# Attention values in one pass of four heads, the compressed branch interleaved with projections, five staging tiles, last sums by part

## The chip, the cores and the metric

The kernel runs on one core of a Trainium2 chip. The metric is the time of one execution in device microseconds (us); a comparison goes by medians of runs. The engines are TensorE (PE in the rows, PEld its weight loads), VectorE (DVE), ScalarE (ACT), GpSimd (POOL) and SyncE (SP), which here only issues transfers. [...]

## What is computed

One layer of a hybrid decoder block for 1024 tokens of width 1024, all in float32, and a last RMSNorm. Cut to what matters here:

```python
h = rmsnorm(x, norm1_g); proj = h @ w_in           # one joint input projection
q, kv, gate, qkv, z, b, a = split(proj)            # 8 NSA heads in 2 groups, 4 GDN heads
k_cmp = rope(kv[:, :, 0])
o_cmp, p = nsa_compressed(q, k_cmp, kv[:, :, 1])   # blocks of 32 tokens every 16, a small MLP:
                                                   #   silu((blk + cmp_pos) @ w1) @ w2
o_slc = nsa_selected(q, k_slc, v_slc, top8(p))     # 64-token blocks chosen by p
o_win = nsa_window(q, k_win, v_win)                # the last 512 tokens
o_nsa = rmsnorm(g0*o_cmp + g1*o_slc + g2*o_win)
o_gdn = gated_deltanet(conv_silu(qkv), b, a) * silu(z)
x = x + concat(o_nsa, o_gdn) @ w_out
x = x + (silu(rmsnorm(x) @ w_gate) * (rmsnorm(x) @ w_up)) @ w_down
return rmsnorm(x, final_g)
```

## The kernel before

**Products in two parts.** Every float32 operand of a large product is split into a high and a low part (`xh`/`xl`, or the two halves of a weight tile), and `split3` (lines 119 to 121) makes one product of three matmuls: high by high, high by low, low by high. `wprep` (L195) brings a weight in: it loads chunks of 512 columns into staging tiles `wraw` (three buffers), ScalarE makes the high part (L205), POOL the low one (L208).

**Order.** The code is written stage by stage, and a scheduler then places the instructions on each engine's queue. Nothing overtakes on a queue. All transfers are issued by SyncE's queue, so a store that waits for its data holds up every load behind it.

**Stages**, with their place in the span. 0 to 61 us: `proj_tok(0)` and `proj_tok(1)`, projections to tokens in rows, eight groups of 24 matmuls each. `proj_tok(0)`'s weights `w0` come with the tiles of x through three staging tiles `xraw`, k by k (L235 to L242); their results go out through `zt` to `zD` (L252, L253). Beside them x is read once more by tokens (`in_xN`, L265) for the norm, and VectorE and ScalarE make sine and cosine of the positions (`ang`, L305; `sn`, L307). 61 to 90 us: `proj_tok(2)`, the keys and values of the compressed branch, whose groups `evac_cmp` (L329) scales into `ck` on ScalarE and rotates on POOL. 90 to 108 us: the compressed branch. `cmp_blocks` transposes the `ck` tiles (L340) and spreads them to `kdt` (L345 on VectorE, L346 on ScalarE); four additions of the block positions (L360) on VectorE; for each of the keys and the values 16 products (L365), a tanh (L369), a small product (L375, L384). 108 to 330 us: `gdn_proj`, twelve gated projections with a convolution on VectorE, the later ones between the GDN chunks' Gram matrices. 330 to 428 us the GDN scan, then the attention's keys. 480 to 785 us: the attention, in 16 units (8 token tiles by 2 groups), of which more below. Then `w_out`, the gate and up projections, and the down projection to 1466 us; after it the sums of squares of the last norm and the result's last tokens.

**Attention units.** `scores(u)` fills probabilities `PC` (compressed), `Pw` (window) and `Ps` (selected) for four heads; `values(u)` (L1029) multiplies them with the values. It takes two heads at a time: for each pair of heads and each key block, TensorE transposes into bank `b` (L1059 for PC, L1065), ScalarE copies the high part to `PT` (L1067), VectorE subtracts the low part (L1068), and TensorE adds products of 256 columns in bank `c` (L1045), of which there is one buffer. After a pair's last block ScalarE copies half of `c` to `otmp` (L1049) and VectorE adds the other half into `mn` (L1050); only then can the next pair's products enter `c`. `merge` weaves the streams of scores, values and output projection (`wob`) by estimated costs `wa` and `wc`.

**Tail.** `norm_sum` (L1606) sums squares over the partitions by products with ones, token chunk by token chunk (L1611), VectorE scales the sum (L1614), POOL takes the power (L1615), TensorE spreads it (L1621), and VectorE and POOL scale the last tokens, which leave in two transfers of 512 KB (L1663).

## Time and profile before

| | |
|---|---|
| median of 3 runs | 1499.25 us (1497.87 to 1504.8) |
| the profiled execution | 1494.86 us |
| its span, first to last instruction | 1493.1 us |
| mean granted clock of TensorE in it | 0.985 |
| TensorE busy | 1426.7 us, 96% |
| VectorE, ScalarE, POOL busy | 65%, 48%, 47% |

The span lies inside the execution's time; all rows below are from this one execution. A busy TensorE is not a TensorE at its peak, since the ends of matmuls are modelled and they overlap: the distance from one start to the next is what one costs. A share in brackets behind a row is idle time of the engine just ahead of it and the instruction that released it.

### The profile page before, as it was taken

The numbers are of one execution on the slowest core, as the hardware profiler recorded it, in microseconds if no ns is written. First come the engines' busy times: TensorE is split into PE (matmuls) and PEld (weight loads), VectorE is DVE, ScalarE is ACT, GpSimd is POOL, SyncE is SP. The second block draws the span as 40 slices with busy tenths as digits, with TensorE's granted clock in tenths as the row PEclk, the third lists the DMA queues.
The fourth block names the chain that finished last, engine by engine and source line by source line (L and its number), as shares of the span: only waits on it lengthen the run. The fifth ranks groups of instructions, "written<-read, shape, count | busy, mean of one in ns | idle before, by whom it ended". The sixth has DMA issues, their size and how long they took to land.

```text
span 1493.1 us, 23452 instructions
## 1 busy us (share of the span) xinstructions
PE 1426.7 (96%) x7984; PEld 1220.1 (82%) x7984; DVE 966.9 (65%) x2286; ACT 723.5 (48%) x1604; POOL 708.1 (47%) x755
## 2 busy tenths in 40 slices
PE   8889999999998999999999999999999999999997
PEld 8878877899987887888887788888888887888886
DVE  4326688826655898998956864444444434999955
ACT  5433356236655888778755543333333332444423
POOL 1232244561121755654467277566666553345435
PEclk9999999999998999999999999999999999999998
DMA  7822255477735313101137123222222237534003
GB/s 250 300 68 78 92 171 162 126 194 208 203 119 202 101 54 107 47 22 44 36 123 244 36 87 99 83 78 85 78 86 85 85 92 274 200 119 134 1 0 113
DMA packets 142743, 174.96 MB, mean 117 GB/s; under 512 B 26912, under 2 KB 79392, under 8 KB 142496
## 3 DMA queue, kind: packets, MB, share of 16 engines
q1 hardware_dynamic: 142624, 173.47, 37.0%
q8 instruction: 63, 1.03, 0.3%
q14 instruction: 56, 0.46, 0.1%
HBM read 122.01 MB, written 51.41 MB: 116 GB/s over the span
## 4 chain that ended last, share of the span: by engine, by line
PE 60%; DVE 10%; issue 5%; ACT 5%; POOL 4%; DMA 2%; SPq 0%; POOLq 0%; ACTq 0%; DVEq 0%
PE mm L119 16%; PE mm L121 16%; PE mm L120 16%; PE c L1045 3%; PE b L1065 2%; DVE PT L1068 2%; ACT Ps L1016 1%; PE a L637 1%; DVE cy L429 1%; PE a L999 1%; PE a L644 1%; ACT PT L1067 1%; DMA wraw<-in_w_out 1%; POOL w L208 1%; DMA mgt<-mgD 1%
## 5 line engine op out<-in xcount | busy, mean ns | idle before, releaser
L1202 POOL TENSOR_TENSOR A<-wq,A 128x512 fp32r<-128x512 f32 x94 | 126.4, 1346 | 97.8 <-ACT A L1201 76.5
L1201 ACT ACTIVATE A<-wq 128x512 fp32r<-128x512 f32 x96 | 60.1, 630 | 135.0 <-PE mm L121 118.3
L119 PE MATMUL mm<-w,xh 128*128 128x256 f32 x384 | 112.2, 292 | 6.3 <-ACT w L205 3.9
L1068 DVE TENSOR_TENSOR PT<-b,PT 128x512 fp32r<-128x512 f32 (+2 forms) x168 | 103.8, 621 | 18.8 <-ACT PT L1067 17.0
L120 PE MATMUL mm<-w,xh 128*128 128x256 f32 x384 | 112.0, 292 | 1.0 <-POOL w L208 1.0
L121 PE MATMUL mm<-w,xl 128*128 128x256 f32 x384 | 111.9, 291 | 0.0
L1202 POOL TENSOR_TENSOR wk<-wq,wk 128x512 fp32r<-128x512 f32 x61 | 82.6, 1355 | 53.0 <-ACT wk L1201 44.7
L1067 ACT ACTIVATE PT<-b 128x512 fp32r<-128x512 f32 (+2 forms) x168 | 89.0, 538 | 37.4 <-PE b L1065 33.2
L1045 PE MATMUL c<-PT,vs 128*128 128x256 f32 x528 | 92.9, 300 | 0.1
L208 POOL TENSOR_TENSOR w<-wraw,w 128x512 fp32r<-128x512 f32 x48 | 63.5, 1337 | 60.6 <-ACT w L205 34.6
L1201 ACT ACTIVATE wk<-wq 128x512 fp32r<-128x512 f32 x63 | 39.6, 630 | 85.4 <-PE mm L121 78.5
L119 PEld LDWEIGHTS mm<-w,xh 128*128 128x128 f32 x384 | 75.3, 196 | 6.9 <-ACT w L205 4.1
L119 PE MATMUL mm<-T,A 128*128 128x512 f32 x200 | 79.2, 396 | 0.0
L120 PE MATMUL mm<-T,A 128*128 128x512 f32 x200 | 79.2, 396 | 0.0
L121 PE MATMUL mm<-T,A 128*128 128x512 f32 x200 | 79.2, 396 | 0.0
L1479 POOL TENSOR_TENSOR ring<-ring,ring 128x512 f32<-128x512 f32 x44 | 58.2, 1324 | 40.1 <-DVE ring L1464 26.5
L120 PEld LDWEIGHTS mm<-w,xh 128*128 128x128 f32 x384 | 75.5, 196 | 1.3 <-POOL w L208 1.2
L119 PE MATMUL mm<-xh,w 128*128 128x512 f32 x192 | 75.7, 394 | 0.0
L121 PEld LDWEIGHTS mm<-w,xl 128*128 128x128 f32 x384 | 75.4, 196 | 0.1
L121 PE MATMUL mm<-xh,w 128*128 128x512 f32 x192 | 75.3, 392 | 0.0
L1045 PEld LDWEIGHTS c<-PT,vs 128*128 128x128 f32 x528 | 73.0, 192 | 2.5 <-DVE PT L1068 0.3
L120 PE MATMUL mm<-xl,w 128*128 128x512 f32 x192 | 74.9, 390 | 0.0
(471 smaller groups left out, 4515.0 us busy)
## 6 DMA issues: line engine op xcount, KB each, us to landing
wq<-in_w_gu SPq DMA_DIRECT2D x92, 256.0 KB, 2.7
aD<-ring SPq DMA_DIRECT2D x44, 256.0 KB, 2.2
ring<-aD SPq DMA_DIRECT2D x44, 256.0 KB, 4.1
raw<-in_w_dn SPq DMA_DIRECT2D x36, 256.0 KB, 3.9
qk<-gD SPq DMA_DIRECT2D x16, 512.0 KB, 4.8
wraw<-in_w_out SPq DMA_DIRECT2D x28, 256.0 KB, 2.8
wraw<-in_w_tok SPq DMA_DIRECT2D x24, 256.0 KB, 2.9
wraw<-in_w_gdn SPq DMA_DIRECT2D x24, 256.0 KB, 2.8
```

The lines of the kernel that those rows point to most:

```text
L119: after(mm(ps, lhsT=lh, rhs=rh, start=first, stop=False, skip_group_check=grow), prev)
L120: mm(ps, lhsT=lh, rhs=rl, start=False, stop=False, skip_group_check=grow)
L121: return mm(ps, lhsT=ll, rhs=rh, start=False, stop=last, skip_group_check=grow)
L208: (lo or G).tensor_tensor(out=wt[:, 1, k0:k0 + n, :], in0=raw, in1=f32(wt[:, 0, k0:k0 + n, :]), op=ALU.subtract)
L429: V.scalar_tensor_tensor(out=y, in0=cr[:, j:j + 512], scalar=cw[:, j:j + 1], in1=y, op0=ALU.mult, op1=ALU.add)
L1045: mm(po[:, 0:256], lhsT=v, rhs=PT[0:K, a, b_ * 256:(b_ + 1) * 256], start=(n_ == 0 and a == 0), stop=(last and b_ == len(vs) - 1 and a == 1))
L1065: tpose(pt[:, o_:o_ + P], src[:, hh, b * P:(b + 1) * P], ident)
L1067: act(out=PT[0:K, 0, 0:w], in_=pt[0:K, 0:w], func=AF.Copy)
L1068: V.tensor_tensor(out=PT[0:K, 1, 0:w], in0=pt[0:K, 0:w], in1=f32(PT[0:K, 0, 0:w]), op=ALU.subtract)
L1201: act(out=dst[:, 0], in_=src, func=AF.Copy)
L1202: after(eng.tensor_tensor(out=dst[:, 1], in0=src, in1=f32(dst[:, 0]), op=ALU.subtract), prev)
L1479: G.tensor_tensor(out=t, in0=half[o], in1=t, op=ALU.mult)
```

## The change

- **Lead.** The first x tile comes as two halves of 512 columns, `w0`'s first weights between them. `xraw` has five buffers, and `w0`'s staging is a tile of its own, `w0raw`, with five. `wprep` has four staging buffers where a caller does not name a number.
- **Compressed branch.** Its weights (`w1t`, 2 MB), `w2t` and `cpt` are loaded ahead of `proj_tok(2)` in the code. `cmp_blocks(i-1)` is called in `evac_cmp(i)`; the additions of positions are 16 of 128x256, half of them on POOL. `gdn_proj(0)` stands before the large products, `gdn_proj(4)` between them and the tanh; both use the earlier pool of banks. The zero stores to `uD` and `tD` come after these.
- **Values.** One pass of four heads for each unit: products of 512 columns, half as many; one copy of 64x512 and two additions at the end of a unit instead of two copies and two additions. `Ps` has four buffers (three before), `qt` and `otmp` one (two before), `wx` is shared with another tile of the same shape.
- **Memory.** Six small tiles move to a pool that closes earlier.
- **Tail.** `norm_sum` goes part by part; for the last tokens each token chunk has a bank of its own, and VectorE scales each. The result's last tokens leave in four transfers of 256 KB, issued by SyncE and ScalarE in turn.

The diff, cut:

```diff
-    def wprep(src, K, w, lo=None, tag="w", bufs=2, pl=None, rawbufs=3, rawpl=None, hi=None):
+    def wprep(src, K, w, lo=None, tag="w", bufs=2, pl=None, rawbufs=4, rawpl=None, hi=None):
...
+    XB = 5
     w0 = mk(p1, [P, 2, KD, TOKW[0]], "w1t", F32R)
     for k in range(KD):
-        r = mk(p1, [P, T], "xraw", F32, 3)
-        dma(r, xT[:, k, :])
-        raw = mk(pw, [P, TOKW[0]], "wraw", F32, 3)
-        dma(raw, tok_src(0)[:, k, :])
+        r = mk(p1, [P, T], "xraw", F32, XB)
+        raw = mk(p1, [P, TOKW[0]], "w0raw", F32, XB)
+        for hf in range(2 if k == 0 else 1):
+            xs = slice(hf * 512, (hf + 1) * 512) if k == 0 else slice(0, T)
+            dma(r[:, xs], xT[:, k, xs])
+            if hf == 0:
+                dma(raw, tok_src(0)[:, k, :])
...
     def evac_cmp(i, ps):
...
+        if i > 0:
+            cmp_blocks(i - 1)
     def cmp_blocks(i):
...
+                for jj in range(2):
+                    pos_j = cpt[:, a, 8 * jj:8 * jj + 8].unsqueeze(2)
+                    for g in range(2):
+                        (V if jj == 0 else G).tensor_tensor(out=kdt[a][jj][:, :, g, n0:n0 + 32],
+                                                            in0=kdt[a][1][:, :, g, n0:n0 + 32],
+                                                            in1=bc(pos_j, [P, 8, 32]), op=ALU.add)
+    w1t = mk(p1, [P, 2, 16, P], "w1t")
+    dma(w1t, cw1)
...
     proj_tok(2, evac_cmp, banka)
-    for i in range(NT):
-        cmp_blocks(i)
+    cmp_blocks(NT - 1)
+    gdn_proj(0, banka)
...
+    gdn_proj(4, banka)
...
-                Ps[hp] = mk(pn, [P, 2, T], "Ps", F32, 3)
+                Ps[hp] = mk(pn, [P, 2, T], "Ps", F32, 4)
...
+        def products(n_, K, v, PT):
+            for a in range(2):
+                mm(po, lhsT=v, rhs=PT[0:K, a], start=(n_ == 0 and a == 0), stop=(n_ == len(blocks) - 1 and a == 1))
...
+        tmp = mk(pn, [64, 512], "otmp", F32, 1)
+        act(out=tmp, in_=po[64:128], func=AF.Copy)
         for hp in range(2):
...
-        return [0.3 + 0.35 + n * 0.3] * 2
+        return [0.6 * (n + 1) + 0.9]
...
-        for j in range(n):
-            for q_, t in enumerate(parts):
+        for q_, t in enumerate(parts):
+            for j in range(n):
...
-    ms = norm_sum(parts, w)
+    ms = norm_sum(parts, w, None, [mk(pps4, [P, 512], "mm", F32, 6) for _ in range(w // P)])
...
-        if dt % 4 == 3:
-            dma(out[:, dt - 3:dt + 1, hf * 512 + o:hf * 512 + o + w], x2[hf][:, dt - 3:dt + 1, o:o + w])
+        if dt % 2:
+            (dma if dt % 4 == 1 else nc.scalar.dma_start)(
+                out[:, dt - 1:dt + 1, hf * 512 + o:hf * 512 + o + w], x2[hf][:, dt - 1:dt + 1, o:o + w])
```

Since a scheduler places the instructions, the diff does not show where they stand; three places follow.

SyncE's queue at the end of `proj_tok(1)`, before. `wraw<-in_w_tok` is a weight chunk of `proj_tok(2)`, `w1t<-in_cw` the 2 MB of the compressed branch, `zD<-zt` a store that waits for ScalarE:

```order
L281 DMA posi_705<-in_pos 128x8
L203 DMA wraw_738<-in_w_tok 128x512
L253 DMA zD_58<-zt_520 128x256
L203 DMA wraw_742<-in_w_tok 128x512
L203 DMA wraw_746<-in_w_tok 128x512
L253 DMA zD_58<-zt_548 128x256
L352 DMA w1t_1054<-in_cw 128x4096
L253 DMA zD_58<-zt_576 128x256
L253 DMA zD_58<-zt_604 128x256
L203 DMA wraw_750<-in_w_tok 128x512
L253 DMA zD_58<-zt_632 128x256
L354 DMA w2t_1056<-in_cw 128x192
```

Three chunks stand ahead of the 2 MB load here, the fourth behind it. The same place on SyncE's queue in the changed kernel:

```order
L388 DMA w1t_738<-in_cw 128x4096
L257 DMA zD_58<-zt_549 128x256
L257 DMA zD_58<-zt_577 128x256
L390 DMA w2t_740<-in_cw 128x192
L257 DMA zD_58<-zt_605 128x256
L392 DMA cpt_742<-in_cpos 128x32
L203 DMA wraw_745<-in_w_tok 128x512
L203 DMA wraw_749<-in_w_tok 128x512
L257 DMA zD_58<-zt_633 128x256
L203 DMA wraw_753<-in_w_tok 128x512
L203 DMA wraw_757<-in_w_tok 128x512
L203 DMA wraw_1078<-in_w_gdn 128x512
```

The 2 MB load has moved ahead of all four chunks, and each chunk now stands behind three or four stores of `zt`.

TensorE from the last transposes of the compressed branch (L340) on, before:

```order
L340 MATMUL b_1038<-cst_75,ck_977 128x128
L340 MATMUL b_1038<-cst_75,ck_1010 128x128
L365 MATMUL mm_1062<-kdt_101_733,w1t_1054 128x126 x8
L365 MATMUL mm_1062<-kdt_102_734,w1t_1054 128x126 x8
L375 MATMUL mm_1085<-hy_1079,w2t_1056 128x126
L365 MATMUL mm_1091<-kdt_103_735,w1t_1054 128x126 x8
L365 MATMUL mm_1091<-kdt_104_736,w1t_1054 128x126 x8
L384 MATMUL mm_1113<-w2t_1056,hy_1108 63x64 x2
```

The branch's steps follow one another with nothing between. TensorE's order in the changed kernel, where L373 is the transpose and `mm<-xh,w` are matmuls of `gdn_proj(0)`:

```order
L373 MATMUL b_985<-cst_75,ck_1014 128x128
L373 MATMUL b_987<-cst_75,ck_1014 128x128
L119 MATMUL mm_1086<-xh_89,w_1077 128x512
L120 MATMUL mm_1086<-xl_90,w_1077 128x512
L373 MATMUL b_987<-cst_75,ck_1049 128x128
L121 MATMUL mm_1086<-xh_89,w_1077 128x512
L373 MATMUL b_985<-cst_75,ck_1049 128x128
L119 MATMUL mm_1086<-xh_89,w_1077 128x512
L120 MATMUL mm_1086<-xl_90,w_1077 128x512
```

The last transposes have moved in among the first matmuls of the projection. Further on on TensorE, L401 are the large products, ahead of which `gdn_proj(0)` ends and behind which `gdn_proj(4)` begins:

```order
L121 MATMUL mm_1123<-xh_89,w_1077 128x512
L401 MATMUL mm_1160<-kdt_101_734,w1t_738 128x126 x8
L401 MATMUL mm_1160<-kdt_102_735,w1t_738 128x126 x8
L401 MATMUL mm_1177<-kdt_103_736,w1t_738 128x126 x8
L401 MATMUL mm_1177<-kdt_104_737,w1t_738 128x126 x8
L119 MATMUL mm_1203<-xh_89,w_1194 128x512
```

Whole projections have come between the branch's own steps.

TensorE in the attention stage, before: the hand-over of bank `c` inside a unit, from one pair of heads (L1045 with `c_1098`) to the next (`c_1112`). L999 are scores of selected keys, L119 to L121 the output projection, L1065 transposes:

```order
L1045 MATMUL c_1098_6060<-PT_1097_6057,vs_892_5143 128x256 x4
L999 MATMUL a_1109_6129<-kss0_788_4406,QS_1030_5773 128x384
L999 MATMUL a_1109_6129<-kss1_789_4407,QS_1030_5773 128x384
L119 MATMUL mm_1087_6007<-mgt_919_5254,wo_1084_6000 128x512
L120 MATMUL mm_1087_6007<-mgt_919_5254,wo_1084_6000 128x512
L121 MATMUL mm_1087_6007<-mgt_919_5254,wo_1084_6000 128x512
L1065 MATMUL b_1110_6142<-cst_15_75,Ps_1064_5927 128x128 x4
L999 MATMUL a_1114_6154<-kss0_788_4406,QS_1030_5773 128x384
L999 MATMUL a_1114_6154<-kss1_789_4407,QS_1030_5773 128x384
L1045 MATMUL c_1112_6150<-PT_1101_6076,vcs_27_91 128x256 x2
```

Nine rows, with some 2 us of matmuls or less, stand between one pair and the next. TensorE in the changed kernel (L1051 for L1045, L956 and L964 scores of the next unit, L1062 transposes), where `c` is handed over between units alone: the last rows ahead of a hand-over, where `c_1154` follows `c_1110`:

```order
L1062 MATMUL b_1164_6396<-cst_15_75,Pw_1122_6201 128x128 x2
L119 MATMUL mm_1160_6374<-mgt_920_5270,wo_1157_6367 128x512
L120 MATMUL mm_1160_6374<-mgt_920_5270,wo_1157_6367 128x512
L121 MATMUL mm_1160_6374<-mgt_920_5270,wo_1157_6367 128x512
L956 MATMUL a_1167_6408<-ksw0_790_4421,QS_1102_6134 128x192
L956 MATMUL a_1167_6408<-ksw1_791_4422,QS_1102_6134 128x192
L964 MATMUL a_1168_6413<-ksw0_790_4421,QS_1102_6134 128x384
L964 MATMUL a_1168_6413<-ksw1_791_4422,QS_1102_6134 128x384
L1062 MATMUL b_1169_6419<-cst_15_75,Pw_1107_6140 128x128 x2
L1062 MATMUL b_1169_6419<-cst_15_75,Pw_1122_6201 128x128 x2
L1051 MATMUL c_1154_6358<-PT_1156_6364,vcs_21_85 128x512 x2
```

The hand-over inside a unit, with few matmuls between, is gone; the one between units has the next unit's first scores and transposes in it.

## Rows read from the trace of the kernel before

**Rows 1.** Windows: attention stage; busy us (instructions) by engine, TensorE clock, DMA share
```profile
480.00:785.00 305.00, 289.00 (x1881) 246.66 (x1878) 256.58 (x1000) 240.37 (x608) 173.03 (x212) 0.99 0.21 68
```

**Rows 2.** Timeline (start, us, instruction, [idle before, releaser]): ScalarE, first us
```profile
5.08 0.72 ACT L242 ACTIVATE xh<-xraw,vec 128x512 fp32r<-128x512 f32 x1 [2.20 <-DMA xraw<-in_xT]
```

**Rows 3.** Timeline, SyncE's queue, around the fourth weight chunk
```profile
53.20 1.43 SPq L352 DMA_DIRECT2D w1t<-in_cw  x1
58.08 3.72 SPq L253 DMA_DIRECT2D zD<-zt  x2
61.90 0.37 SPq L203 DMA_DIRECT2D wraw<-in_w_tok  x1
```

**Rows 4.** Timeline, ScalarE, the same stretch
```profile
60.77 0.26 ACT L307 ACTIVATE sn<-ang 128x64 f32<-128x64 f32 x1 [1.42 <-DVE ang L306]
...
61.08 0.64 ACT L252 ACTIVATE zt<-mm 128x256 f32<-128x256 f32 x2
64.99 0.63 ACT L205 ACTIVATE w<-wraw 128x512 fp32r<-128x512 f32 x1 [3.27 <-DMA wraw<-in_w_tok]
```

**Rows 5.** Timeline, VectorE and POOL, the angles' steps
```profile
56.91 0.22 DVE L305 SCALAR_TENSOR_TENSOR ang<-nh,ang 128x64 f32<-128x64 f32 x1
...
57.03 2.51 POOL L208 TENSOR_TENSOR w<-wraw,w 128x512 fp32r<-128x512 f32 x2 [1.40 <-ACT w L205]
...
57.17 1.23 DVE L305 SCALAR_TENSOR_TENSOR ang<-nn,ang 128x64 f32<-128x64 f32 x1
```

**Rows 6.** Timeline, TensorE, third projection's start
```profile
65.67 0.38 PE L119 MATMUL mm<-w,xh 128*128 128x256 f32 x1 [3.92 <-ACT w L205]
...
68.25 0.42 PE L119 MATMUL mm<-w,xh 128*128 128x256 f32 x1
...
72.73 0.32 PE L119 MATMUL mm<-w,xh 128*128 128x256 f32 x1
```

**Rows 7.** Timeline, TensorE, compressed branch and next projection
```profile
90.27 0.28 PE L121 MATMUL mm<-w,xl 128*128 128x256 f32 x1
90.39 1.03 PE L340 MATMUL b<-cst,ck 128*128 128x128 f32 x8
93.47 1.06 PE L340 MATMUL b<-cst,ck 128*128 128x128 f32 x8 [2.04 <-ACT kdt L346]
97.17 5.22 PE L365 MATMUL mm<-kdt,w1t 128*128 128x126 f32 x32 [2.64 <-DVE kdt L360]
103.08 0.49 PE L375 MATMUL mm<-hy,w2t 128*128 128x126 f32 x2 [0.69 <-DVE hy L370]
103.40 3.74 PE L365 MATMUL mm<-kdt,w1t 128*128 128x126 f32 x32
...
108.54 0.39 PE L120 MATMUL mm<-xl,w 128*128 128x512 f32 x1
108.77 0.40 PE L121 MATMUL mm<-xh,w 128*128 128x512 f32 x1
```

**Rows 8.** Groups of the attention stage, VectorE (count | busy, mean ns)
```profile
L1068 DVE TENSOR_TENSOR PT<-b,PT 128x512 fp32r<-128x512 f32 x126 | 86.1, 686 | 12.2 <-ACT PT L1067 10.8
...
L1050 DVE TENSOR_TENSOR mn<-c,otmp 64x256 f32<-64x256 f32 x30 | 12.4, 412 | 1.8 <-ACT otmp L1049 1.4
...
L1068 DVE TENSOR_TENSOR PT<-b,PT 64x256 fp32r<-64x256 f32 x29 | 11.9, 409 | 4.1 <-ACT PT L1067 3.8
```

**Rows 9.** Waits of TensorE, attention stage: total, times, longest
```profile
PE c L1045 <- DVE mn L1050: 4.4, 7, 1.2
```

**Rows 10.** Waits of VectorE inside the attention stage
```profile
DVE PC L944 <- PE a L943: 4.9, 6, 2.3
```

**Rows 11.** Timeline, all engines, last sums
```profile
1482.47 0.97 PE L1611 MATMUL n<-ones,gu 128*128 128x2 f32 x4
1483.56 0.16 DVE L1614 TENSOR_SCALAR ms<-n 128x2 f32<-128x2 f32 x1 [1.45 <-PE n L1611]
```

**Rows 12.** DMA engines, last 10 us in 40 slices: GB/s
```profile
GB/s 377 393 303 8 0 61 340 356 352 332 352 254 307 344 360 344 340 291 357 348 348 307 344 365 328 348 348 352 336 348 226 0 0 0 0 0 0 0 0 0
```

More of the change, by code (lines that the diff above doesn't have):

```diff
@@ L356, in hybrid_block @@
     dma(cpt, cpos)
+    proj_tok(2, evac_cmp, banka)
+    cmp_blocks(NT - 1)
+    gdn_proj(0, banka)
+    pshs = {}
     for a in range(2):
-        for j in range(2):
-            pos_j = cpt[:, a, 8 * j:8 * j + 8].unsqueeze(2)
-            V.tensor_tensor(out=kdt[a][j].rearrange("p r g n -> p r (g n)"),
-                            in0=kdt[a][1].rearrange("p r g n -> p r (g n)"), in1=bc(pos_j, [P, 8, P]), op=ALU.add)
-        psh = banka("mm")
+        psh = pshs[a] = banka("mm")
         hv = psh[:, 0:2 * NCMP].rearrange("p (g n) -> p g n", g=2)
@@ L408, in hybrid_block @@
     pg, pg_x = pool("pg")
[L410 to L434 removed]
     for h in range(4):
[L437 to L438 removed]
+        if h:
+            gdn_proj(h, bank)
+            gdn_proj(4 + h, bank)
     pgs, pgs_x = pool("pgs", side="right")
@@ L556, in hybrid_block @@
             gram(c)
-        gdn_proj(8 + h)
+        gdn_proj(8 + h, bank)
     V.tensor_scalar(ssq, ssq, 4.0 * EPS, None, op0=ALU.add)
@@ L865, in prep_q @@
     def prep_q(i, g):
-        qt = mk(pk, [P, 256], "qt", F32, 2)
+        qt = mk(pk, [P, 256], "qt", F32, 1)
         dma(qt, qD[g, i])
@@ L1026, in hybrid_block @@
     LAG = 3
-    WXB = 2
     def values(u):
@@ L1074, in values @@
-        for fn, a_ in todo:
-            fn(*a_)
-            yield 0.3
+        Pw, Ps = u["Pw"], u["Ps"]
+        blocks = [None] + [(Pw, b, VS[:, i - np_ + b, 2 + g, :]) for b in range(np_ + 1)]
+        blocks += [(Ps, b, VS[:, b, g, :]) for b in range(i + 1)]
+        po = bank("c")
+        def products(n_, K, v, PT):
+            for a in range(2):
+                mm(po, lhsT=v, rhs=PT[0:K, a], start=(n_ == 0 and a == 0), stop=(n_ == len(blocks) - 1 and a == 1))
+        for n_, blk in enumerate(blocks):
+            pt = bank("b")
+            for h in range(4):
+                if blk is None:
+                    K, v = 64, vcs[:, g, :]
+                    tpose(pt[0:64, h * P:(h + 1) * P], PC[:, h, 1:65], ident)
+                else:
+                    src, b, v = blk
+                    K = P
+                    tpose(pt[:, h * P:(h + 1) * P], src[h // 2][:, h % 2, b * P:(b + 1) * P], ident)
+            PT = mk(pn, [P, 2, 512], "PT", F32R, LAG + 1)
+            act(out=PT[0:K, 0], in_=pt[0:K], func=AF.Copy)
+            V.tensor_tensor(out=PT[0:K, 1], in0=pt[0:K], in1=f32(PT[0:K, 0]), op=ALU.subtract)
+            todo.append((n_, K, v, PT))
+            if len(todo) > LAG:
+                products(*todo.pop(0))
+            yield 0.6
@@ new lines, in values @@
+        for a_ in todo:
+            products(*a_)
+            yield 0.3
+        tmp = mk(pn, [64, 512], "otmp", F32, 1)
+        act(out=tmp, in_=po[64:128], func=AF.Copy)
+        for hp in range(2):
+            V.tensor_tensor(out=mn[hp * 64:(hp + 1) * 64, g * 2:g * 2 + 2, i * P:(i + 1) * P],
+                            in0=po[0:64, hp * 256:(hp + 1) * 256].rearrange("p (h t) -> p h t", h=2),
+                            in1=tmp[:, hp * 256:(hp + 1) * 256].rearrange("p (h t) -> p h t", h=2), op=ALU.add)
```

122 lines of the change are left out of this document (43 added, 79 removed).

## The prediction

> **What bounds the kernel now.** I read the waits of TensorE over the whole span first, then the timelines around the longest of them, then the grouped costs of the attention stage. For nearly all of the span TensorE is the engine that everything waits for, so a microsecond that TensorE stands idle or runs at the low clock early on is a microsecond of the total; the places to look at are those where it does not work. The change touches five of them. At the start ScalarE waits 2.20 us for the first tile of x [rows 2]. At 61 us TensorE stands 3.92 us for the last chunk of weights of the compressed keys' projection [rows 6]. From 90 to 108 us it stands at every step of the compressed branch [rows 7]. In the attention stage, 305 us long, TensorE shows 289.00 us busy, VectorE 256.58 and ScalarE 240.37 [rows 1]: both first engines are nearly full, so neither alone sets the time. At the end TensorE is done and the result's transfers fill the DMA engines [rows 12].
>
> **The lead.** The first x tile comes in two halves, with the weights between them. Of ScalarE's 2.20 us wait [rows 2] a half can go, about 1 us, since half the bytes are asked for; nothing makes it longer. But what follows 34 us later is a wait for weights that come from their own chain (next part), so TensorE arrives there earlier only to wait longer. I take 0, with 1 us of gain as the other end.
>
> **Weights of the compressed keys' projection.** Before, the four chunks of w L205/L208 are loaded well before their use but for the fourth: SyncE has two stores zD<-zt ahead of it, which it enters at 58.08 and leaves at 61.8, so the chunk is issued at 61.90 [rows 3] and ScalarE starts on it at 64.99 [rows 4]. The stores wait for zt on ScalarE, which at 60.77 had waited 1.42 us for ang of VectorE and only then made zt at 61.08 [rows 4]. TensorE had done 18 of the first group's 24 matmuls with three chunks; it begins group 2 at 68.25 and goes at the lower clock, 1.2 GHz, until 72.73 [rows 6].
> In the new order the 2 MB load w1t stands ahead of all four chunks, and all four stand behind the store of the very zt that follows sin on ScalarE (the order of SyncE in the section on the change). So the three chunks that were early are now late too. What comes out of that I count from rows. POOL's two conversions no longer run at 57.03, and VectorE's steps on ang took 1.23 us beside them instead of 0.22 [rows 5]; there are two such slow steps, so ang comes 2 us earlier, and three conversions of 0.63 us leave ScalarE's way. The first chunk is then issued near 60, and lands 3.1 us later (61.90 to 64.99), at 63.1. ScalarE's high part takes 0.63 us; POOL's low parts come one behind the other at 2.51/2 = 1.26 us each: 65.0, 66.3, 67.5, 68.8. The first group ends with six more matmuls at 69.5, against 68.25 before: 1.2 us later. The low clock: before, 21 matmuls from 68.25 to 72.73 took 0.213 us each instead of 0.12, 2.0 us lost; TensorE stands as long in the new order, so the clock falls again; if it rises at the same time, 15 matmuls lose 1.4 us, 0.6 less than before. Net +0.6; with the clock back by 69.5 it is -0.8. I take +0.3, nearer to the first. The ends: -2.5 if the chunks come 2 us earlier than counted, +4 if ang comes no earlier and the clock stays low as long as before.
>
> **The compressed branch.** Transposes go between the token groups, the position additions are cut into sixteen pieces on VectorE and POOL, and one gated projection each (some 11 us of TensorE: 48 matmuls of 512 columns at 0.23 us [rows 7]) stands before the big products and between them and the last ones. What goes: the waits of 2.04 and 2.64 us, the low clock of the first half of the products, 5.22 - 3.74 = 1.48 us, and two waits of 0.69 us, one of them shown: 7.5 us in all [rows 7]. Their cover is real: the additions, whose last one ended the 2.64 us wait and half of which are now POOL's, have 11 us of projection over them; without that cover the 2.64 us would be back. What comes: the last two transposes follow only two matmuls behind their group while their input passes ScalarE and POOL, and the next projection's first bank waits for the last reads of the branch, since the pool of banks changes right there. Neither is in the trace; the nearest row is a hop over ScalarE and VectorE with 0.69 us of wait [rows 7], so two times 0.65 = 1.3 us, between 0 (hidden) and 2.5 (both at twice that). So -6.2, between -5.0 and -7.5. The zero stores of uD and tD now share SyncE's queue with the gated weights; they are wanted in later stages, and the weights of the next projection are asked for ahead of them, so I put it at nothing; the projection running above them hides it, and without it a wait like the 3.92 us would come back.
>
> **Values in one pass.** The products were 592 of 256 columns and are 296 of 512. A 256-column step is 0.12 us (90.27 to 90.39), a 512-column step 0.23 (108.54 to 108.77) [rows 7]: 71.0 against 68.1 us, -2.9 on TensorE. VectorE: 32 subtractions of 64x256 at 0.409 and 8 of 128x256 taken alike, 16.4 us, become 20 of 512 columns at 0.686, 13.7 us: -2.7 [rows 8]. ScalarE's copies shrink alike and are not the bound. The bank c has one buffer; its release to the next pass costs TensorE 4.4 us in 7 waits [rows 9]. Passes were 32 and are 16. In the orders, counted at the steps above, 1.1 to 2.1 us of other matmuls stand between the passes inside a unit, and only between units 3.2 to 5.3 us; the new passes are all between units, with 3.2 to 5.5 us but for the first and last. The bank is now held for a 64x512 copy and two additions of 0.412 us [rows 8], some 1.5 us: it fits, and the 4.4 us can go. By TensorE the stage thus gains 7.3, by VectorE 2.7. Both are nearly full [rows 1], so I take the middle, -5. The ends: -9 with some of ScalarE's relief on top, and +1 if VectorE's order alone decides and the reordering costs a little. The further moves (qt and otmp to one buffer, wx to a shared pool, Ps to four) have no wait in the trace that they would lengthen or end; nothing.
> [...]
>
> **The tail.** The last sums are taken part by part, so that behind the last square two products stand instead of four; two of them took 0.97 us [rows 11], of which I count half as the spacing of one behind the other. With a second small step on VectorE for the second bank, 0.4 us is saved. VectorE had stood 1.45 us at that step with the scaling of the other tiles behind it [rows 11], so their transfers start 0.4 us earlier too, and from there the DMA engines move 250 to 370 GB/s to the end [rows 12]. Four transfers on two queues carry the same bytes: nothing. -0.4, between -0.8 and +0.5 (more, smaller transfers).
> The page "DMA: Bandwidth & Descriptors" of the Trainium skill, on issuing engines, says that transfers issued from several engines run on the same 16 DMA engines and save only the time of issue; by it the second queue brings nothing, and the full rates of that row agree.
>
> **Sum.** 0 + 0.3 - 6.2 - 5.0 - 0.4 = -11.3 us. The profiled execution took 1494.86 us (1493.1 of span), so 1483.6 by it; it lies 4.4 us under the median of the runs, 1499.25, which is what is compared: 1488.0.
>
> **The rivals.**
> Late weights: the 2 MB load and the chain over ang hold all four chunks, at +4 instead of +0.3. For it speaks the order of SyncE; against it that ang loses its slow steps. -7.6, 1491.6.
> Attention gains nothing: VectorE's and ScalarE's chain between transposes and products sets the pace, and TensorE only waits elsewhere. For it speak 256.58 us of VectorE; against it the 4.4 us of waits that are plainly TensorE's. -6.3, 1493.
> Slower: at the start of each unit VectorE waits for the first scores. Such waits took 4.9 us in 6 times, the longest 2.3 [rows 10]. With the passes joined, a unit's last products come in one run ahead of the next unit's scores, and each of the 16 units may pay it. At the mean, 0.82 us, 16 x 0.82 - 4.9 = +8.2 in place of -5 makes +1.9 in all, no difference; at 1.55, halfway to the longest, +19.9 makes +13.6, 1513. It decides from 1.2 us per unit. Against it speaks that in the new order the next unit's scores stand ahead of its first products as before.
> Better: chunks 2 us earlier and attention by TensorE's count: -2.5 - 6.2 - 7.3 - 0.4 = -16.4, 1483.
>
> **How the numbers follow.** A measurement of this kernel tells about 0.5%, 7.5 us, from no change. Forecast 0.50 (own range 1484 to 1492), better 0.12, late weights 0.14, no gain in attention 0.16, slower 0.08. Faster than 1491.8 are all of better, nearly all of the forecast (0.46), and a bit over a third of late weights (0.05): 0.63; within 0.5% is the rest but for slower: 0.29; slower 0.08. The range leaves out slower and 0.05 at either side: 1478 to 1497.
>
> **What would show it.** Right: no TensorE wait over 1 us from the last token group to the gated projections, the branch's products at full clock; c waits under 1 us; in the stage TensorE and VectorE both some 3 us less busy. Weights: TensorE's second group of the compressed keys near 69.5; under 68 or over 71 would make that step wrong. Tail: last end 0.4 us nearer to the last square. Wrong altogether: new waits over 1 us at the start of most units, or waits of the gram stage that swallow what came earlier.

## The result and the profile after

The changed kernel takes 1482.3 us (median of 4 runs, 1479.44 to 1483.71) against 1498.83 us of the kernel before (4 runs): a ratio of 0.989, 95% interval 0.9862 to 0.9919. In two later series it took 1483.9 and 1482.3 us, ratios 0.9897 (0.9868 to 0.9926) and 0.9884 (0.9861 to 0.9907). So it is faster by 1.1%, inside the range and 5.7 us under the predicted time.

The profiled execution took 1483.71 us (span 1482.0, mean clock 0.989), against 1494.86. The page shows TensorE's busy time 7.5 us down, VectorE's 2.8:

```profile
span 1482.0 us, 22842 instructions
...
PE 1419.2 (96%) x7688; PEld 1195.6 (81%) x7688; DVE 964.1 (65%) x2271; ACT 716.8 (48%) x1568; POOL 713.0 (48%) x763
```

Where the two profiled executions come apart is read from the starts of the same TensorE instructions in the two timelines:

| TensorE starts | before | after | difference |
|---|---|---|---|
| end of the second projection | 57.65 | 60.36 | +2.7 |
| second group of the third projection | 68.25 | 69.44 | +1.2 |
| fifth group of the third projection | 78.87 | 78.64 | -0.2 |
| third gated projection | 130.11 | 122.80 | -7.3 |
| first scores of the attention | 459.59 | 452.91 | -6.7 |
| first product with values | 469.19 | 463.28 | -5.9 |
| last product with values | 781.46 | 767.45 | -14.0 |
| end of gate and up projections | 1251.74 | 1238.64 | -13.1 |
| last large product | 1480.32 | 1469.79 | -10.5 |
| end of the span | 1493.1 | 1482.0 | -11.1 |

**The lead** became longer, which no part of the prediction had. ScalarE's timeline in the first 10 us of the kernel after (start, duration, instruction, idle time ahead and its releaser):

```profile
4.66 0.44 ACT L242 ACTIVATE w1t<-w0raw 128x288 fp32r<-128x288 f32 x1 [1.72 <-DMA w0raw<-in_w_tok]
5.01 0.71 ACT L246 ACTIVATE xh<-xraw,vec 128x512 fp32r<-128x512 f32 x1
6.25 0.72 ACT L246 ACTIVATE xh<-xraw,vec 128x512 fp32r<-128x512 f32 x1 [0.53 <-DMA xraw<-in_xT]
9.08 0.72 ACT L246 ACTIVATE xh<-xraw,vec 128x512 fp32r<-128x512 f32 x1 [2.11 <-DMA xraw<-in_xT]
```

ScalarE's first wait, now for the weights and not for x as in [rows 2], is 0.48 us shorter, but the second tile of x is worked on at 9.08, after a new wait of 2.11 us. Before, ScalarE went on to the second tile without a wait. TensorE starts 0.4 us earlier (5.77 for 6.18) and then stands for it; its longest wait behind the start (total, times, longest):

```profile
PE mm L119 <- ACT w1t L242: 2.1, 1, 2.1
```

Besides, 26 of its first steps take 0.24 us instead of 0.13, against 19 before: some 0.8 us more. Wait and slow steps, less the early start, make up nearly all of the 2.7 us.

**The weights.** SyncE's queue and ScalarE, to be held against [rows 3] and [rows 4]; then TensorE at the third projection, against [rows 6]:

```profile
59.38 0.86 SPq L203 DMA_DIRECT2D wraw<-in_w_tok  x2
60.74 0.33 SPq L257 DMA_DIRECT2D zD<-zt  x1
61.17 0.88 SPq L203 DMA_DIRECT2D wraw<-in_w_tok  x2
```
```profile
57.92 0.26 ACT L311 ACTIVATE sn<-ang 128x64 f32<-128x64 f32 x1 [0.70 <-DVE ang L310]
...
62.10 0.63 ACT L205 ACTIVATE w<-wraw 128x512 fp32r<-128x512 f32 x1 [2.37 <-DMA wraw<-in_w_tok]
```
```profile
60.36 1.95 PE L277 MATMUL b<-cst,rstd 128*128 128x128 f32 x16
62.78 0.38 PE L119 MATMUL mm<-w,xh 128*128 128x256 f32 x1 [0.47 <-ACT w L205]
...
69.44 0.28 PE L119 MATMUL mm<-w,xh 128*128 128x256 f32 x1
```

All four chunks now stand behind stores, as the order had said, and `sn` comes 2.85 us sooner. The 3.92 us wait is now one of 0.47 us and four short ones of 2.5 us together.

**The branch.** The waits of TensorE from 60 to 110 us (total, times, longest), the whole list, and its timeline at the first projections behind the branch, against [rows 7]:

```profile
PE mm L120 <- POOL w L208: 2.5, 4, 1.0
PE mm L119 <- ACT w L205: 0.5, 1, 0.5
PE b L373 <- POOL ck L326: 0.5, 1, 0.5
```
```profile
103.31 7.30 PE L401 MATMUL mm<-kdt,w1t 128*128 128x126 f32 x64
122.80 0.50 PE L119 MATMUL mm<-xh,w 128*128 128x512 f32 x1 [0.66 <-DVE kcl L417]
```

The four waits and the slow half of the products are gone: 64 products in 7.30 us, where before 32 took 5.22 and 32 took 3.74.

**The attention.** A row of the windows view (busy us and count of each engine, then clock, DMA share and GB/s) from the first to the last product with values, of before and of after, and TensorE's waits there in the kernel after, against [rows 9]:

```profile
469.20:781.40 312.20, 296.69 (x1916) 253.86 (x1916) 264.26 (x1043) 246.09 (x636) 171.16 (x211) 0.98 0.23 75
```
```profile
463.30:767.40 304.10, 286.95 (x1616) 230.10 (x1616) 263.29 (x1019) 238.04 (x596) 171.35 (x211) 0.99 0.24 76
```
```profile
PE a L956 <- DVE mx L970: 5.8, 8, 1.3
PE a L1012 <- DVE mx L1022: 4.0, 4, 2.2
...
PE c L1051 <- DVE mn L1076: 0.2, 1, 0.2
```

The 4.4 us of waits for bank `c` are 0.2. In their place TensorE waits for banks of scores (`a`), which VectorE has still to read.

**The tail**, timeline of all engines, against [rows 11]:

```profile
1471.25 1.03 PE L1615 MATMUL mm<-ones,gu 128*128 128x2 f32 x8
...
1472.17 0.31 DVE L1620 TENSOR_SCALAR ms<-mm 128x1 f32<-128x1 f32 x2 [0.59 <-PE mm L1615]
...
1475.73 1.19 SPq L1671 DMA_DIRECT2D out<-B  x2
1476.18 1.32 ACTq L1671 DMA_DIRECT2D out<-B  x2
```

### The profile page after: what moved, and what is told of

It is laid out like the page before. It is cut to its first block, busy times and chain, and to the rows that moved or that the text cites. A ratio compares the mean times of both kernels' runs of the same rounds, so it can differ in the third digit from the quotient of the medians.

```text
span 1482.0 us, 22842 instructions
## 1 busy us (share of the span) xinstructions
PE 1419.2 (96%) x7688; PEld 1195.6 (81%) x7688; DVE 964.1 (65%) x2271; ACT 716.8 (48%) x1568; POOL 713.0 (48%) x763
## 4 chain that ended last, share of the span: by engine, by line
PE 59%; DVE 10%; issue 6%; POOL 4%; ACT 4%; DMA 4%; SPq 1%; POOLq 0%; DVEq 0%; ACTq 0%
PE mm L119 16%; PE mm L121 16%; PE mm L120 16%; PE c L1051 2%; DVE PT L1065 2%; PE b L1062 1%; PE a L650 1%; PE a L1012 1%; DVE cy L353 1%; DMA wraw<-in_w_out 1%; ACT PT L1064 1%; ACT Ps L1029 1%; PE a L657 1%; POOL sqa L1646 1%; DVE Ps L1022 1%
## 5 line engine op out<-in xcount | busy, mean ns | idle before, releaser
L119 PE MATMUL mm<-w,xh 128*128 128x256 f32 x384 | 111.3, 290 | 2.8 <-ACT kst L593 2.3
L1065 DVE TENSOR_TENSOR PT<-b,PT 128x512 fp32r<-128x512 f32 (+1 forms) x148 | 101.0, 685 | 18.0 <-ACT PT L1064 17.2
L121 PE MATMUL mm<-w,xl 128*128 128x256 f32 x384 | 110.5, 288 | 0.0
L1064 ACT ACTIVATE PT<-b 128x512 fp32r<-128x512 f32 (+1 forms) x148 | 86.1, 589 | 29.8 <-PE b L1062 28.2
L1051 PE MATMUL c<-PT,vs 128*128 128x512 f32 x264 | 89.5, 425 | 0.1
L119 PE MATMUL mm<-T,A 128*128 128x512 f32 x200 | 79.1, 396 | 0.0
L121 PE MATMUL mm<-T,A 128*128 128x512 f32 x200 | 79.1, 396 | 0.0
L119 PEld LDWEIGHTS mm<-w,xh 128*128 128x128 f32 x384 | 74.2, 193 | 3.5 <-ACT kst L593 2.5
L119 PE MATMUL mm<-xh,w 128*128 128x512 f32 x192 | 75.9, 395 | 0.7 <-DVE kcl L417 0.7
L1513 DVE TENSOR_TENSOR B<-B,mm 128x512 f32<-128x512 f32 x100 | 63.8, 679 | 19.2 <-PE mm L121 15.7
L121 PE MATMUL mm<-xh,w 128*128 128x512 f32 x192 | 75.3, 392 | 0.0
L121 PEld LDWEIGHTS mm<-w,xl 128*128 128x128 f32 x384 | 74.3, 193 | 0.1
```

The source lines that it names most:

```text
L119: after(mm(ps, lhsT=lh, rhs=rh, start=first, stop=False, skip_group_check=grow), prev)
L121: return mm(ps, lhsT=ll, rhs=rh, start=False, stop=last, skip_group_check=grow)
L1051: mm(po, lhsT=v, rhs=PT[0:K, a], start=(n_ == 0 and a == 0), stop=(n_ == len(blocks) - 1 and a == 1))
L1064: act(out=PT[0:K, 0], in_=pt[0:K], func=AF.Copy)
L1065: V.tensor_tensor(out=PT[0:K, 1], in0=pt[0:K], in1=f32(PT[0:K, 0]), op=ALU.subtract)
L1513: V.tensor_tensor(out=out_, in0=a_, in1=b_, op=op)
```

## The experiments

Each kernel is the changed one with the edits shown. Executions of one kernel lie 3 to 15 us apart, along with the mean granted clock that each was given: 39 executions of the kernel before go from 1490.04 us (clock 0.987) to 1504.87 (0.978), and a straight line through them makes a run 1.3 us shorter for each 0.001 of clock; through the 16 of the changed kernel it is 1.2. So the medians tell about 4 us apart, and smaller questions are put to the timelines, with the time counted for which the profile shows a granted clock of 0.5, 1.2 GHz.

**Values as before** (only the pass over heads and its costs restored):

```diff
-        po = bank("c")
-        def products(n_, K, v, PT):
-            for a in range(2):
-                mm(po, lhsT=v, rhs=PT[0:K, a], ...)
+        for hp in range(2):
+            ...
+                        mm(po[:, 0:256], lhsT=v, rhs=PT[0:K, a, b_ * 256:(b_ + 1) * 256], ...)
```

> The changed kernel, but the attention's values are again made two heads at a time with products of 256 columns, and the planner's cost of them is the old one; Ps keeps its four buffers, everything else is as changed. In the changed kernel's profile the stretch from the first to the last value product is 304.2 us, before it was 312.3. Theory: the joint pass itself gives this, by wider products (2.9 us) and by the waits for bank c (4.4 us before, 0.2 now): here the stretch is 311 to 313 us again, the wait for c 3 to 5 us, and the run about 8 us longer than the changed kernel. Rival: the fourth Ps buffer lets the next unit's scores run ahead, and that gives most of it: the stretch stays under 307 us and the run within 3 us of the changed kernel.

Measured: 1484.82 us (7 runs, 1483.26 to 1491.02), 0.9936 of before (0.9907 to 0.9964). That is 2.5 us over the changed kernel's first median where the theory had 8, but the seven had different clocks, 0.985 to 0.991. At one clock, 0.988, they lie at 1487.2, the 16 executions of the changed kernel at 1482.5: 4.7 us.

The timelines say the same. From the first scores to the last product with values it takes 319.6 us here, 10.2 of them at 1.2 GHz. The five profiles of the joint pass that have 10.2 us at 1.2 GHz in this stretch, the changed kernel and its first repeat among them, take 314.5 to 315.8: the joint pass is worth 3.8 to 5.1 us. The kernel before, 321.9 with 17.1 us at 1.2 GHz, stands 4.4 over the two profiles of the joint pass with 17.1. Here `Ps` keeps its fourth buffer, and yet the stretch is as much longer as in the kernel before: the rival falls. From the first product alone the difference is larger, 310.0 against 304.2 us, because the part ahead of it, from the first scores on, is longer in the changed kernel's profile (10.4 us for 9.6 here). The windows rows from the first scores on (values as before, then the changed kernel) and TensorE's longest waits of the first:

```profile
450.34:769.97 319.63, 300.85 (x1954) 255.88 (x1952) 271.48 (x1094) 253.86 (x668) 172.99 (x213) 0.98 0.25 81
```
```profile
452.91:767.45 314.54, 294.50 (x1657) 236.68 (x1656) 270.83 (x1073) 246.19 (x631) 172.80 (x213) 0.98 0.25 83
```
```profile
PE c L1057 <- DVE mn L1062: 4.5, 7, 1.2
PE a L956 <- DVE mx L970: 2.2, 5, 0.7
```

With the same time at 1.2 GHz TensorE's busy time falls by 6.3 us, VectorE's by 0.7, and TensorE's idle time grows from 18.8 to 20.0 (over the five: 5.5 to 6.4, 0.2 to 0.9, and 1.2 to 1.7 more idle time). The waits for `c` come back with the old pass; removing them did not remove TensorE's idle time.

**Branch as before** (transposes after the projection, whole additions on VectorE, no projections between, and with that the 2 MB load behind the chunks again):

```diff
-        if i > 0:
-            cmp_blocks(i - 1)
...
     proj_tok(2, evac_cmp, banka)
-    cmp_blocks(NT - 1)
-    gdn_proj(0, banka)
+    for i in range(NT):
+        cmp_blocks(i)
```

> The changed kernel with the compressed branch in the old order: transposes after the whole projection, additions in four pieces on VectorE, no gated projections between, its weights asked for after the projection's; five staging tiles, the values and the tail as changed. Theory: the waits of the branch (2.0, 2.6, 0.7 and 0.7 us) and 1.5 us of low clock come back, from the first transposes to the first gated projection it takes 17 to 18 us, and the third gated projection starts 6 to 7 us later than in the changed kernel, less what the earlier weight chunks give (the old order of loads): with both, 3 to 7 us longer than the changed kernel. Rival: the gain up to the gated projections comes from the start and the loads; then this run is within 2 us of the changed kernel.

Measured: 1487.47 us (8 runs, 1483.38 to 1489.99), 0.993 of before (0.9905 to 0.9956), 5.2 us over the changed kernel's first median, within the 3 to 7 of the theory. The waits of the branch are back in TensorE's timeline:

```profile
87.38 1.06 PE L371 MATMUL b<-cst,ck 128*128 128x128 f32 x8 [2.04 <-ACT kdt L377]
91.08 6.45 PE L396 MATMUL mm<-kdt,w1t 128*128 128x126 f32 x32 [2.63 <-DVE kdt L391]
98.22 0.49 PE L406 MATMUL mm<-hy,w2t 128*128 128x126 f32 x2 [0.69 <-DVE hy L401]
```

From the fifth group of the third projection to the third gated projection it takes 52.4 us, against 44.2 in three profiles of the changed kernel and 51.2 in the kernel before. Of the 8.3 us 1.2 are a longer low clock under the first 32 products, 6.45 for 5.22 us. So the interleaving is worth 7.1 us.

**The 2 MB load behind the chunks:**

```diff
+    cpt = mk(p1, [P, 2, 16], "cpt")
+    dma(cpt, cpos)
+    proj_tok(2, evac_cmp, banka)
     w1t = mk(p1, [P, 2, 16, P], "w1t")
...
-    proj_tok(2, evac_cmp, banka)
     cmp_blocks(NT - 1)
```

> The changed kernel, with one thing moved: the loads of w1t (2 MB) and w2t stand after the third projection in the code, so that SyncE issues its four weight chunks ahead of the 2 MB load. In the changed kernel the first group of that projection waits for the chunks one by one and its second group starts at 69.4 us, 9 us after the second projection's end. Theory: the wait is one of the order of loads alone; here the second group starts 5 to 6 us after the second projection's end, near 66, and all that follows comes 3 to 4 us earlier, to the end. Rival: the chain over the positions' angles on VectorE and the low parts on POOL slow each other again, the rotation of the keys becomes late, and the gain is under 1 us or lost in the compressed branch.

Measured: 1480.99 us (5 runs), 0.9889 (0.9859 to 0.9919); in its profile the wait for weights is gone, the third gated projection starts at 117.75 instead of 122.80, and the span is 5.8 us shorter. The median moved by 1.3. To settle which of the two holds, the changed kernel and this one were run again, side by side:

> The changed kernel once more, five rounds, as the mark that the next two runs are held against on the same chip. 1481 to 1484 us, as its two earlier medians (1482.3 and 1483.9).

> The 2 MB load behind the four chunks of weights, five rounds. Theory A, the order of loads costs the changed kernel 5 us, as the milestones of the first profile say (the third gated projection 5.05 us earlier): at least 3 us under the changed kernel of the same call, 1476 to 1480. Theory B, what is gained there is given back to later waits and to the clock, as the medians say (1480.99 against 1482.3): less than 2 us apart.

Measured: 1482.3 us (6 runs, 1479.79 to 1485.64) and 1481.86 (6 runs, 1478.64 to 1483.91). Theory B: the order of the loads makes no difference that these runs can tell. In this second profile of the late load the third gated projection stands at 119.73, not 117.75, because a wait has grown where the other went; TensorE's waits from 55 to 100 us in the first profile, the second, and the changed kernel run beside it:

```profile
PE b L373 <- POOL ck L326: 1.0, 2, 0.6
```
```profile
PE b L373 <- POOL ck L326: 3.0, 2, 2.6
```
```profile
PE mm L120 <- POOL w L208: 2.1, 4, 1.0
PE b L373 <- POOL ck L326: 0.5, 1, 0.5
PE mm L119 <- ACT w L205: 0.4, 1, 0.4
```

The transposes wait for POOL's rotation of `ck`, which needs `sn`. With the chunks early, two steps on `ang` take 1.20 and 1.05 us again instead of 0.22, and `sn` begins 1.8 us ahead of the second projection's end in the first profile and 0.3 in the second; in the three profiles of the changed kernel it is 2.4 to 2.8. So the rival of the first of these runs holds in part: some of what the early chunks give goes to a late rotation.

**Three staging tiles instead of five, with the late load:**

```diff
-    XB = 5
+    XB = 3
```

> The same as the run before it, and also three staging tiles in place of five for x and its weights at the start (the first tile still in two halves). In the changed kernel the second projection ends at 60.2 us, 2.7 later than before, although TensorE starts 0.4 earlier: ScalarE waits 2.1 us for the second tile of x, and TensorE's clock rises at 15.9 us and not at 11.2. Theory: with five tiles more transfers are under way at once and share the DMA engines, so the second tile lands later; with three the second tile is there by 7 us, the second projection ends near 57.2, and this run is 2.5 to 3 us under the run before it, 6 to 7 under the changed kernel. Rival: it is the halving of the first tile (three transfers ahead of the second tile in place of two) that delays it; then ScalarE's wait of 2 us stays and nothing is gained over the run before.

Measured: 1487.5 us (9 runs, 1481.2 to 1492.33), 0.993 (0.9904 to 0.9956). With three tiles the transposes' wait is

```profile
PE b L373 <- POOL ck L326: 5.5, 2, 5.1
```

so the gain of the load's place is lost altogether. The second projection ends at 60.02, no earlier than with five tiles (58.78 to 60.36 in eight profiles): they are not what made the lead longer, and that theory falls. `sn` begins at 60.88, only behind the second projection's end; with five tiles and the same order of loads it was 57.14 and 58.58. Why the angles come later with three tiles was not tried.

**The changed kernel again**, on the chip of the next three:

> The changed kernel itself once more, with more runs. So far its runs read 1479 to 1484 us and those of before 1490 to 1505, and within one kernel a run is longer where its mean granted clock is lower (before: 1490.0 us at 0.987, 1504.9 at 0.978). Theory: the difference of the medians, 16.5 us, holds the difference in the work (11 us in the two profiles) and one in how long the clock was low in the runs. Expected 1480 to 1484 in the median, and the low clock in other places of this profile than in the first.

Measured: 1483.9 us (6 runs, 1479.55 to 1485.89). Its profile starts the third gated projection at 121.31 and spans 1482.2.

**The first tile whole:**

```diff
-        for hf in range(2 if k == 0 else 1):
-            xs = slice(hf * 512, (hf + 1) * 512) if k == 0 else slice(0, T)
+        for hf in range(1):
+            xs = slice(0, T)
```

> The changed kernel, but the first tile of x is loaded whole again; five staging tiles as changed. So far ScalarE began the second tile of x at 6.8 us before (three tiles, whole), 8.1 us with three tiles and the first one halved, and 8.4 and 9.1 with five and halved. Theory: the halved first tile delays the second one most; here ScalarE begins it at 6.8 to 7.4 us, TensorE's wait of 1.3 to 2.1 us at 8 us is gone, and the second projection ends at 57 to 58 us. Rival: five tiles under way at once are the cause, and the second tile comes at 8 us or later here too. Either way the third projection's wait for its weights, which hangs on other transfers, takes most of it: the third gated projection starts within 2 us of the changed kernel's 122.7.

Measured: 1481.38 us (6 runs), 0.9884 (0.9857 to 0.9912). ScalarE is at the second tile at 6.94 instead of 9.08 (and 8.07 with three tiles and halves):

```profile
5.00 0.72 ACT L246 ACTIVATE xh<-xraw,vec 128x512 fp32r<-128x512 f32 x1 [2.29 <-DMA xraw<-in_xT]
...
6.94 0.72 ACT L246 ACTIVATE xh<-xraw,vec 128x512 fp32r<-128x512 f32 x1 [0.27 <-DMA xraw<-in_xT]
```

The second projection ends at 57.74, as in the kernel before; the two other profiles with a whole tile have 57.95 and 58.68, the eight with halves and five tiles 58.78 to 60.36, 59.3 in the mean against 58.1. So the halves cost some 1.2 us, and 2.6 in the first profile. The bytes are the same, but the DMA engines carry them slower: from 4 to 6 us 246 to 285 GB/s in those eight, 363 to 387 in the three with a whole tile. Windows from 4 to 8 us, last two columns DMA share and GB/s, of the changed kernel and of the whole tile:

```profile
4.00:6.00 2.00, 0.23 (x1) 0.23 (x2) 0.70 (x2) 1.06 (x2) 0.00 (x0) 1.00 0.85 260
6.00:8.00 2.00, 2.00 (x8) 1.74 (x8) 1.25 (x2) 0.72 (x1) 0.00 (x0) 1.00 0.91 268
```
```profile
4.00:6.00 2.00, 0.00 (x0) 0.00 (x0) 0.24 (x1) 1.00 (x3) 0.00 (x0) 1.00 1.05 387
6.00:8.00 2.00, 1.89 (x7) 1.81 (x8) 1.84 (x4) 1.45 (x4) 0.00 (x0) 1.00 0.97 327
```

What is lost here is carried on in full: the changed kernel, its repeat and this one end the second projection at 60.36, 58.78 and 57.74 and start the third gated projection at 122.80, 121.31 and 120.24. No wait takes it in, because the chunks of weights move with it: here they are issued between 55.32 and 58.03, ScalarE starts on the first at 58.37, and the second group begins at 66.74.

**Both, whole tile and late load**, once on that chip and once beside the runs above:

> The run before with the 2 MB load behind the weight chunks too, as in the run of that edit, where the third projection no longer waited. Theory: with no wait left there, an earlier end of the second projection comes through: the third gated projection starts 1 to 1.5 us earlier than the 117.6 of that run, and the whole is 6 to 7 us under the changed kernel in the profile. Rival: the chain over the angles is no earlier than before, so the keys' rotation on POOL now waits, as it did with three tiles (5.1 us there), and nothing is gained over that run.

> The first tile of x whole and the 2 MB load behind the chunks. If the two gains add, some 2 us under the run with the late load alone; if the projection's wait takes the first one in, as its first profile said (third gated projection 118.19 against 117.61), the same as that within 1.5 us.

Measured: 1478.91 us (6 runs, 1475.5 to 1483.72), 0.9867 (0.9839 to 0.9895), the lowest median of all; and then 1481.89 (6 runs), 0.9878 (0.9854 to 0.9903), the same as the late load alone beside it. In the first profile the transposes' wait takes 2.6 us and the third gated projection starts at 118.33, no earlier than the late load alone had it in one of its profiles: the two gains do not add. Over all executions the changed kernel has 16 with a median of 1483.1 us, the late load 11 with 1481.2, both together 12 with 1480.3. A gain of 2 to 3 us is possible, and not shown.

**Tail as before** (one bank, sums chunk by chunk, two transfers):

```diff
-        for q_, t in enumerate(parts):
-            for j in range(n):
+        for j in range(n):
+            for q_, t in enumerate(parts):
...
-        if dt % 2:
-            (dma if dt % 4 == 1 else nc.scalar.dma_start)(
+        if dt % 4 == 3:
+            dma(
```

> The changed kernel with the old tail: last sums chunk by chunk in one bank, two transfers of 512 KB from SyncE. From the last matmul of the down projection to the end of the span it is 12.9 us before and 12.3 in the changed kernel. Theory: the order of the sums gives 0.4 to 0.6 us, the four transfers on two queues nothing: here 12.7 to 13.0 us. Rival: the transfers are what gives it, or nothing does: 12.3 or under. No run can show this in its total.

Measured: 1481.96 us (6 runs, 1479.07 to 1483.15), 0.9885 (0.986 to 0.9911): the same as the changed kernel. In the timelines the last large product starts 12.5 us ahead of the end of the span, 12.2 in the changed kernel and its repeats, 12.8 in the kernel before. From the start of the last product with ones on it is 10.0 us in all of them (10.05 before, 10.00 here, 9.95 in the changed kernel), so the difference lies ahead of it, in the sums, and not in the transfers. The tail is worth 0.3 to 0.6 us, less than the runs can tell.

## Why the prediction was right, and where it was not

**The sum by the profile** was 1483.6 us and the profiled execution took 1483.71. The two agree so closely because misses of opposite sign cancel: taken from mark to mark of the table, the lead is +2.7 where I had 0, the weights -2.9 where I had +0.3, the branch -7.1 for -6.2, the values -8.1 for -5.0; then 1.4 us are given back between the third gated projection and the first product with values, 0.9 up to the end of gate and up, 2.6 in the down projection, for none of which I had a term; the end makes -0.6. That is luck. **The step that failed for the time itself is the last one:** I added the 4.4 us by which the profiled execution of before lay under its median, as if they belonged to the kernel. Most of them were the clock of one execution. It had 0.985, the median over 39 executions of the kernel before is 0.983, and the line through them makes 2.6 us of that; another 0.8 is that the median of the three runs lay over that of the 39, 1498.42. The profiled execution of after lay 1.4 us over its first median, and there the clock explains nothing: it had 0.989, the median over 16 is 0.988. The 5.7 us of the miss are these two offsets, 4.4 + 1.4, less the 0.1 of the sum.

The clock is also a part of the gain, for which the sum had a term in two places only. At one clock, 0.988, the two lines give 1491.3 and 1482.5 us: 8.8 us of the 15.3 between the medians of all executions (1498.4 and 1483.1). The rest goes with the higher clock of the changed kernel, 0.988 for 0.983. Over the spans of the first profiles 44.8 and 32.4 us lie at 1.2 GHz. Two such stretches of before are gone in the profile after: one from 66.0 us, right behind the 3.92 us wait, and one from 96.7, in the branch. What else raises the clock was not tried.

**The lead: wrong in sign.** I had written that nothing makes it longer. The whole-tile run shows what does. I priced the half by its bytes alone and not by what the halves do to the transfers behind them: the second tile came 2.1 us later. The Trainium skill's "Perfetto Trace Analysis", on DMA optimizations, says that splitting may let a task finish sooner when the DMA engines are generally idle; here they were 85 and 91% busy with the halves and 105 and 97% with the whole tile, its condition was not met, and the tile behind the halves came later. My second half fails too: an earlier TensorE would not wait longer for the weights, since their chunks stand behind stores of what TensorE has just made, and come earlier with it.

**The weights: the mark right, by two errors.** The second group was predicted at 69.5 and stands at 69.44, but 2.7 us of that are the lead. With the whole tile it stands at 66.74, in the repeats at 67.94 and 67.66, under the 68 from which I had called the step wrong. The chunks stand behind the stores as the order had said, and yet do not come late: `ang` lost its slow steps (the rival of late weights had named that as what speaks against it), and `sn` came early enough. From the end of the second projection to the fifth group of the third it takes 21.2 us before, 18.3 after and 18.4 with the whole tile: -2.9, just beyond the -2.5 that I had kept as the end "if the chunks come 2 us earlier". The 1.4 us of low clock that I had counted are not there either: the clock is full in this stretch, and in the first repeat, where it was at 1.2 GHz for 3.4 us from 64.1 on, the stretch takes 18.3 all the same. That the number of staging tiles bears on the angles, as the 5.1 us wait with three suggests, I had not weighed.

**The branch: right.** -6.2 predicted, between -5.0 and -7.5; measured -7.1 from mark to mark, and the same by the run with the old branch. New waits were put at 1.3 us; they are 0.5 (transposes for POOL's `ck`) and 0.66 (the next projection's first bank), 1.2 in all, at the two places named. What went was 0.8 us more than the 7.5 counted.

**The attention: right in sum, wrong in parts, and so in part by luck.** -5 was the middle between TensorE's count of 7.3 and VectorE's of 2.7; at equal clock it is -3.8 to -5.1. (The -8.1 between the marks hold the clock as well: from the first scores on before has 17.1 us at 1.2 GHz, after 10.2.) But TensorE's 7.3 were 2.9 of products and 4.4 of waits, and it is 5.5 to 6.4 of busy time and nothing of waits: its idle time grew by 1.2 to 1.7. The product term was too small because I took one step for all products. Those with the compressed values have 64 rows; two of them take 0.43 us at 256 columns before and 0.66 at 512 after (TensorE's timelines of before and of after):

```profile
522.76 0.50 PE L1045 MATMUL c<-PT,vcs 64*128 64x256 f32 x2
523.19 0.50 PE L951 MATMUL a<-ksw,QS 128*128 128x256 f32 x2
```
```profile
514.57 0.73 PE L1051 MATMUL c<-PT,vcs 64*128 64x512 f32 x2
515.23 0.50 PE L964 MATMUL a<-ksw,QS 128*128 128x256 f32 x2
```

So 64 at 0.215 become 32 at 0.33: 3.2 us saved where 0.12 and 0.23 had given 0.3. The ordinary ones, with 128 rows, take the steps that I had used, 0.119 and 0.232, behind another product or behind scores; behind a transpose, where most runs of them begin, they take 0.20 and 0.315. In the mean, with waits left out, 528 at 0.137 become 264 at 0.265: 2.4 us. Together that is 5.6, what TensorE's busy time shows. The wait term was too large because a wait on one bank was counted as TensorE's to keep: VectorE reads the scores no faster, and TensorE meets it at bank `a` instead. Nor was VectorE "nearly full": 256.58 of 305 us are 84%. Its own 2.7 did come from the subtractions and went elsewhere. By group, of the values as before and then of the repeat (count, busy, mean ns):

```profile
L1080 DVE TENSOR_TENSOR PT<-b,PT 128x512 fp32r<-128x512 f32 (+2 forms) x167 | 103.4, 622 | 17.6 <-ACT PT L1079 16.2
...
L1034 DVE TENSOR_TENSOR gr<-gr,gate 128x2 f32<-128x2 f32 x30 | 7.1, 238 | 0.2
```
```profile
L1065 DVE TENSOR_TENSOR PT<-b,PT 128x512 fp32r<-128x512 f32 (+1 forms) x147 | 100.3, 684 | 17.3 <-ACT PT L1064 16.5
...
L1034 DVE TENSOR_TENSOR gr<-gr,gate 128x2 f32<-128x2 f32 x30 | 10.2, 343 | 0.1
```

3.1 us off the subtractions, 3.1 us onto a product of 128x2 that is unchanged but slower. Why it is slower was not tried. Of the rivals, "attention gains nothing" had the right mechanism, the chain over VectorE takes back what TensorE's waits free, but not its size. "Slower" fell: VectorE's waits for the first scores are 3.3 us in 2 times, not one in each of 16 units.

**The tail: right**, -0.4 predicted, 0.3 to 0.6 by the timelines; second queue and smaller transfers show nothing. The 0.97 us of [rows 11] are four products, not two as I had read; half of them, which I counted, is what two take.

**The down projection's 2.6 us** were in no rival. TensorE waits there for weights in both kernels, and in the profile after it goes at the low clock from 1244.6 on (windows rows, clock the third column from the end):

```profile
1238.00:1244.60 6.60, 4.82 (x20) 3.25 (x18) 2.42 (x3) 1.15 (x2) 3.59 (x4) 1.00 0.70 242
1244.60:1251.60 7.00, 5.88 (x14) 4.63 (x15) 1.77 (x2) 2.83 (x5) 5.28 (x4) 0.52 0.86 285
```

The profile before and the second repeat have none of this, the first repeat half as much. So the changed kernel goes either way; whether the kernel before does too, one profile cannot show.

## What to carry to other kernels

Convert a sum over profile steps into a time by the clock as well: where executions of one kernel differ in it, an offset between one profile and a median must not be added to the next kernel. A wait on a buffer is worth its length only if the engine that frees the buffer is not the one that the waiting engine meets at the next buffer. And before halving a first transfer, look at whether the DMA engines are full: what stands behind it pays.

## What was not expected of the hardware

A matmul with 64 rows of weights took 0.215 us at 256 columns and 0.33 at 512, about 0.1 us more than one with 128 rows behind another product (0.119 and 0.232), so joining such products saves more than their columns say. One with 128 rows right behind a transpose took 0.20 and 0.315. And two transfers of 256 KB in place of one of 512 KB at the start left the DMA engines at 246 to 285 GB/s from 4 to 6 us in eight profiles, where the whole one had 363 to 387 in three; the tile behind the halves was worked on at 8.19 to 9.08 us, behind the whole one at 6.94, 7.30 and 8.26.
